# Ends of the modulation rounds at normal priority, and the recurrence's added products head beside head

## The chip, the cores and the metric

One core of a Trainium2 chip runs the whole program: two network blocks of two layers each, over 256 latent tokens (and 256 context tokens) of width 1024, all in f32. The metric is the device time of one execution in microseconds (us). Engines: PE (TensorE, matrix products; PEld is its weight load), DVE (VectorE), ACT (ScalarE), POOL (GpSimd), SP (SyncE, which issues most of the loads). The 16 DMA engines move data between memory and the core.

## The reference, cut to what matters

Every layer `i` of both blocks is steered by modulations: six rows of 1024 numbers, worked out from a conditioning vector with a weight of 1024 x 6144. The first layer's mixer holds a recurrence (RWKV-7) over the tokens, once forward and once backward, for eight heads of 64 x 64 state.

```
m_lat = jnp.split((c_lat_act @ w_ada[i] + b_ada[i])[:, None, :], 6, axis=-1)
m_ctx = jnp.split(c_ctx_act @ w_ada[i] + b_ada[i], 6, axis=-1)
...
def step(S, inp):
    r_t, w_t, k_t, v_t, a_t, b_t = inp
    sa = jnp.einsum('bhvk,bhk->bhv', S, a_t)
    S = S * w_t[:, :, None, :] + sa[..., None] * b_t[:, :, None, :] + v_t[..., None] * k_t[:, :, None, :]
    return S, jnp.einsum('bhvk,bhk->bhv', S, r_t)
```

The second block's layers use `ada_w` and `ada_b` in the same way. The four layers need 4 x 6 rows; a round makes two of them.

## The kernel before

**Modulations.** `ADA` lists 12 rounds, three for each of four layers: a round is `ada_round(i, r)`, and makes 2048 columns. It loads the weight in 8 steps of two buffers of 128 x 1024 (512 KB each, `raw`, five buffers in this part of the program), from SP's queue (`ada_load`, line 353). In each step four products of 128 x 512, side by side in four column strips of the array, add into one PSUM bank `ps` (line 377). Then comes the end of the round: the bank is added to a row tile `rows` that already holds the bias (line 380, DVE; the tile was cleared by POOL in line 364 and filled by line 373, SP); the sums go to memory as `mrows` for the later gates (line 383, ScalarE's queue; not for the rounds with r = 0); four transposes bring them into columns (line 386, PE) and four small copies into `mcol` (line 391, DVE). The banks of tag "A" hold both the sums and the transposes, and there is one of them; the row tile "adar" has one buffer too. So a round's products can't start before the end of the round ahead of it.

**Where the rounds run.** The first round runs at the start. The other eleven are written ahead of the recurrence (`in_proj`, lines 708 to 711): `filler(999)` issues them all, under `high_priority(offset=APRI)` with APRI = -100000, and then `rwkv()` is issued.

```
        s.fill = ADA[1:NADA]
        with s.tc.high_priority(offset=APRI):
            s.filler(999)
        s.run(s.rwkv())
```

The framework orders the instructions of each engine before the program runs: it follows a planned timeline, and of the instructions of an engine that are ready by it, it picks the one with the earliest place. `high_priority` moves that place forward by its offset; a negative offset moves it back. So the rounds' instructions stand behind all of the recurrence that is ready, and fill in where it is not. On the chip each engine then works through its fixed order, and waits where an operand is late. That goes for SP's queue of loads too, which also has the recurrence's own moves (lines 765, 768, 1018, 1022).

**The recurrence.** `rwkv` works on eight items: two halves of the tokens (th), two halves of those (sh), and two groups of four heads (u). `ORDER` gives their phases: P prepares (decays, keys, scores), I and Q invert small triangular blocks on DVE, C runs the chain `rw_chain`, F finishes. A chain has two steps, `rw_step` (line 1048), 16 in all; the two groups u don't depend on each other. `M` is the state, of the step before; it is absent in the first step of each group. A step has three stretches of products on PE, with copies on ACT and DVE between them:

- `zA`, first half (lines 1065 to 1071): for each direction d and half j, the products of M for both heads, then those of EA for both heads. They are 64 x 64, and stand at the rows of the array of one head and the columns of the other.
- `zA`, second half (lines 1077 to 1079).
- `z` (lines 1084 to 1090): for each d and j, and each of two heads h, a product with the full array from S and, where M is there, a 64 x 64 product from M that is added to half of the partitions of the same result.

All of a stretch lies in one PSUM bank. The step ends with `new = z + new` on DVE (line 1095). All `mm` calls are recorded under line 274; in the trace every f32 product of this kind shows as two instructions.

**Behind it.** `rw_end` and `mixer_out` (line 1369) split the results and project them; their loads stand behind the modulations' in SP's queue, and the gates that `mixer_out` needs are read back from `mrows` (line 414).

Of the kernel before, what the change touches and what calls it, by code (L numbers as in the profile page):

```python
# [12 lines left out]
ALU = mybir.AluOpType  # L13
# [41 lines left out]
APRI = -100000  # L55
# [10 lines left out]
class Builder:  # L66
# [205 lines left out]
    def mm(s, out, **kw):  # L272
        s.work += kw["rhs"].free_size() / (600 if kw["lhsT"].free_size() > 64 else 1200)
        s.nc.tensor.matmul(out, **kw)
# [85 lines left out]
    def ada_round(s, i, r):  # L360
        nc = s.nc
        act = s.act[i // 2]
        rows = s.row(nm="adar")
        nc.gpsimd.memset(rows, 0.0)
        while len(s.fraw) < 2:
            s.ada_load()
        ps = s.ps("ada")
        for k in range(8):
            s.ada_load()
            if k == 2:  # L370
                bsrc = s.I["b_ada" if i < 2 else "ada_b_2"][i % 2:i % 2 + 1, r * 2048:(r + 1) * 2048].rearrange("o (j f) -> (o j) f", j=4)
                for v in range(2):
                    nc.sync.dma_start(rows[v::32, :], bsrc)
            yield
            x = s.fraw.pop(0)
            for j in range(4):
                nc.tensor.matmul(ps[32 * j:32 * j + 32, :], lhsT=act[:, k, :], rhs=x[j // 2][:, j % 2 * 512:j % 2 * 512 + 512],  # L377
                                 start=(k == 0), stop=(k == 7), tile_position=(0, 32 * j))
            x = None
        nc.vector.tensor_tensor(rows, ps, rows, op=ALU.add)  # L380
        yield
        for v in range(0 if r == 0 else 2 if i == 0 else 1):
            nc.scalar.dma_start(s.mrows[i][r, :, v], rows[v::32, :])
        pt = s.ps("adat")
        for b in range(4):
            nc.tensor.transpose(pt[:, b * 128:(b + 1) * 128], rows[:, b * 128:(b + 1) * 128], s.ident)

        src = pt.rearrange("p (b j q) -> p b j q", b=4, j=4)[:, :, :, 0:2]
        dst = s.mcol[i][:, r * 16:(r + 1) * 16, :].rearrange("p (j b) i -> p b j i", j=4)
        for b in range(4):  # L390
            nc.vector.tensor_copy(dst[:, b], src[:, b])
        yield

    now = None

    def filler(s, n):

        while n or s.now:
            if s.now is None:
                if not s.fill and not s.rounds:  # L400
                    return
                s.now = s.ada_round(*(s.rounds or s.fill)[0])
            if next(s.now, s_end) is s_end:
                s.now = None
                s.rounds.pop(0)
            elif n:
                n -= 1
                if not n:
                    return
# [241 lines left out]
    def in_proj(s, xH, xL):  # L651
        nc, I = s.nc, s.I
        W = I["mix_w_in"]
        z13, t0, t1 = s.misc
        s.tl = [t0, t1]

        def ev(j, p):
            if j == 0:
                z12 = s.row(nm="z12")
                s.shift_mix(12, p, z12)  # L660
                for d in range(2):
                    for o in (32, 96):
                        nc.gpsimd.memset(s.tl[d][o:o + 1, :], 1.0)
                    nc.scalar.activation(s.tl[d][0:32, :], z12[32 * d:32 * d + 32, :], AF.Tanh)
                    nc.vector.tensor_copy(s.tl[d][64:96, :], z12[64 + 32 * d:96 + 32 * d, :])
            else:
                s.shift_mix(13, p, z13)

                nc.scalar.activation(z13[0:96, :], z13[0:96, :], AF.Tanh, scale=0.5)
                nc.gpsimd.tensor_scalar(z13[0:96, :], z13[0:96, :], 0.5, 0.5, op0=ALU.mult, op1=ALU.add)  # L670
        s.run(s.wstat2(I["wi_misc"], xH, xL, ev))
        s.z13 = z13
        s.rkv = {}
        s.rw_init()

        def krv_proj(half):
            for nm, o in (("k", 512), ("r", 0), ("v", 1024)):
                if nm == "k":
                    for th in range(2):
                        s.KR[th, half] = s.unit(nm="KR").rearrange("p (x j t) -> p x j t", x=2, j=2)  # L680
                if nm == "v":
                    t = s.rkv["v", half] = s.mx.tile([128, 2, 512], F32, name=s.n("rkv"))
                    z = lambda j: t[:, j]
                else:
                    z = lambda j: [s.KR[th, half][:, int(nm == "r"), j] for th in range(2)]
                yield from s.wstat2(W[:, o + half * 256:o + half * 256 + 256], xH, xL,
                                    lambda j, p: s.shift_mix(o // 128 + half * 2 + j, p, z(j)))
                if nm == "k":
                    s.rw_kk(half)

        s.xbc = [s.unit(nm="xbc").rearrange("p (a t) -> p a t", a=2) for _ in range(4)]
        s.xbc = [x[:, a] for x in s.xbc for a in range(2)]
        s.dump("@xbc")
        for c in range(4):
            s.run(s.wstat2(W[:, 2272 + c * 256:2272 + c * 256 + 256], xH, xL,
                           lambda j, p: s.conv5(c * 2 + j, p, s.xbc[c * 2 + j])))

        s.zg = [s.unit(nm="zg").rearrange("p (a t) -> p a t", a=2) for _ in range(2)]
        s.zg = [x[:, a] for x in s.zg for a in range(2)]

        def z_proj():
            yield from s.xstat(W, slice(1760, 2272), xH, xL, range(4), lambda t, p: nc.scalar.activation(s.zg[t], p, AF.Silu))
        s.dump("@weave")
        s.weave((s.hot(s.mamba(), HOTM), WB[0]), (s.chain(krv_proj(0), z_proj(), krv_proj(1)), WB[1]))
        xH = xL = None
        s.wstop()
        s.dump("@ada")
        s.fill = ADA[1:NADA]
        with s.tc.high_priority(offset=APRI):
            s.filler(999)  # L710
        s.run(s.rwkv())
        s.dump("@s7")
        s.rw_end()
# [334 lines left out]
    def rw_step(s, th, sh, u, i, new):  # L1048

        nc = s.nc  # L1050
        v, a, g = nc.vector, nc.scalar, nc.gpsimd
        mm = s.mm
        Y, M = s.YS[th, u], s.M[u]
        lc = (i, 1 - i)
        ch = (2 * sh + i, 3 - 2 * sh - i)
# [8 lines left out]
        AR, S, EA, UV = s.AR[th, sh, u], s.S[th, sh, u], s.EA[th, sh, u], s.UV[u]  # L1064
# [8 lines left out]
        if M is not None:  # L1073
            q = lambda x: x.rearrange("p h j d t -> p (h j d) t")
# [9 lines left out]
        z = s.ps("Z2").rearrange("p (h j d t) -> p h j d t", h=2, j=2, d=2)  # L1084
        for d, j in dj:
            for h in range(2):
                mm(z[:, h, j, d], lhsT=S[d][:, 2 * j + lc[d], 2 * h:2 * h + 2].rearrange("p e t -> p (e t)"), rhs=UV[:, j, ch[d], h], start=True, stop=True)
                if M is not None:
                    mm(z[BS[h], h, j, d], lhsT=AR[HS[h], d, j, lc[d], 1], rhs=M[HS[h], h, j, d], start=False, stop=True,
                       tile_position=(64 * h, 64 - 64 * h), skip_group_check=True)  # L1090
        f = lambda x: x.rearrange("p h j d t -> p (h j d t)")
# [1268 lines left out]
```

## Time and profile before

| | |
|---|---|
| timed runs (3) | 2815.34, 2804.44, 2808.48 us; median 2808.48 |
| profiled execution | 2815.26 us, span 2813.5 us |
| mean granted TensorE clock | 0.945 |
| instructions | 40633 |
| busy: PE, DVE, ACT, POOL | 93%, 67%, 46%, 6% of the span |

A busy share is a mean over stages that differ. The recurrence's stage lies between 250 and 690 us. A row of the trace has the start and the busy time in us, engine, line, operation and tiles (written <- read); "Z" is the tile of `zA` and `z`, "YM" that of M, "UV" and "S" are the operands of the full products, "EA" that of the other half-size ones.

### The profile page before, as it was taken

What the parts mean: (1) busy time and instruction counts of PE and PEld (TensorE: products, weight loads), DVE (VectorE), ACT (ScalarE), POOL (GpSimd) and SP (SyncE); (2) the same over time, 40 slices, a digit from 0 to 9 for tenths busy, and PEclk for the clock granted to TensorE, in tenths of its full rate; (3) what the DMA queues carried; (4) which work ended last, traced back from release to release, by engine and by line L of the source; (5) the groups of instructions that cost most, each with busy time, mean ns of one, the idle gap of its engine ahead of it and who ended that gap; (6) DMA issues with size and microseconds to landing.
All of it is one profiled execution on the core that took longest, in us unless ns stands there. A gap on an engine that the chain in (4) does not pass through costs nothing. (4 is left out here: it accounts for less than half of the span.)

```text
span 2813.5 us, 40633 instructions
## 1 busy us (share of the span) xinstructions
PE 2623.4 (93%) x15434; PEld 2094.0 (74%) x15434; DVE 1885.7 (67%) x3039; ACT 1287.7 (46%) x1760; POOL 171.5 (6%) x276
## 2 busy tenths in 40 slices
PE   6999899997999998999999999999998987997798
PEld 3776456553888887887788888888876866996797
DVE  4657877833634448456798988898896566555655
ACT  3532122111432223444688777777775443443343
POOL 0112222210000000000000000000000000000000
PEclk8999887887999999999899999999999998998899
DMA  6224776667433333333599999999996324653552
GB/s 238 87 75 161 271 242 195 205 212 276 136 97 98 98 91 105 85 111 112 207 369 349 343 346 344 364 362 340 359 343 238 122 92 148 189 186 99 162 183 75
DMA packets 324444, 570.83 MB, mean 203 GB/s; under 512 B 61752, under 2 KB 167608, under 8 KB 324240
## 3 DMA queue, kind: packets, MB, share of 16 engines
q1 hardware_dynamic: 304064, 544.61, 56.4%
q10 hardware_dynamic: 16784, 11.74, 1.4%
q0 software_dynamic: 3392, 11.80, 1.2%
q8 instruction: 123, 2.02, 0.3%
q14 instruction: 81, 0.66, 0.1%
HBM read 563.79 MB, written 4.28 MB: 202 GB/s over the span
## 5 line engine op out<-in xcount | busy, mean ns | idle before, releaser
L204 DVE TENSOR_TENSOR wl<-raw,wh 128x1024 fp32r<-128x1024 f32 x828 | 984.7, 1222 | 421.7 <-ACT wh L203 401.9
L203 ACT CAST wh<-raw 128x1024 fp32r<-128x1024 f32 x828 | 838.7, 1050 | 506.6 <-issue 191.7
L249 PE MATMUL ws<-xL,wh 128*128 128x256 f32 (+1 forms) x1392 | 456.3, 328 | 3.7 <-DVE xL L204 3.7
L248 PE MATMUL ws<-xH,wh 128*128 128x256 f32 (+1 forms) x1392 | 458.1, 331 | 0.8 <-DVE xTf L482 0.5
L250 PE MATMUL ws<-xH,wl 128*128 128x256 f32 (+1 forms) x1392 | 457.3, 329 | 0.9 <-DVE wl L204 0.9
L249 PE MATMUL mw<-wl,eH 128*128 128x512 f32 (+1 forms) x768 | 289.7, 377 | 1.4 <-DVE wl L204 1.2
L248 PEld LDWEIGHTS ws<-xH,wh 128*128 128x128 f32 x1392 | 265.3, 191 | 33.3 <-issue 7.8
L249 PEld LDWEIGHTS ws<-xL,wh 128*128 128x128 f32 x1392 | 265.1, 190 | 30.7 <-DVE xL L204 4.8
L248 PE MATMUL mw<-wh,eH 128*128 128x512 f32 (+1 forms) x768 | 286.1, 375 | 1.8 <-ACT wh L203 1.8
L250 PEld LDWEIGHTS ws<-xH,wl 128*128 128x128 f32 x1392 | 265.1, 190 | 29.7 <-issue 5.3
L250 PE MATMUL mw<-wh,eL 128*128 128x512 f32 (+1 forms) x768 | 286.2, 373 | 0.0
L377 PE MATMUL ada<-raw,act 128*32 128x512 f32 x768 | 175.0, 731 | 35.2 <-DMA raw<-in_w_ada 14.3
L249 PEld LDWEIGHTS mw<-wl,eH 128*128 128x128 f32 x768 | 145.0, 189 | 33.2 <-DVE wl L204 8.9
L248 PEld LDWEIGHTS mw<-wh,eH 128*128 128x128 f32 x768 | 144.9, 189 | 28.2 <-ACT wh L203 3.1
L250 PEld LDWEIGHTS mw<-wh,eL 128*128 128x128 f32 x768 | 145.0, 189 | 24.0
L249 PE MATMUL y<-wl,uH 128*128 128x512 f32 x352 | 139.6, 397 | 2.0 <-DVE wl L204 2.0
L250 PE MATMUL y<-wh,uL 128*128 128x512 f32 x352 | 135.7, 391 | 0.0
L248 PE MATMUL y<-wh,uH 128*128 128x512 f32 x352 | 115.0, 390 | 0.0
L471 PE MATMUL xT<-ident,xn 128*128 128x128 f32 x160 | 36.0, 403 | 82.8 <-DVE xn L449 51.5
L377 PEld LDWEIGHTS ada<-raw,act 128*32 128x32 f32 x768 | 28.2, 122 | 108.1 <-issue 37.7
L248 PE MATMUL o<-wh,mH 128*128 128x512 f32 x256 | 100.0, 390 | 0.0
L249 PE MATMUL o<-wl,mH 128*128 128x512 f32 x256 | 99.9, 390 | 0.0
(483 smaller groups left out, 4066.4 us busy)
## 6 DMA issues: line engine op xcount, KB each, us to landing
raw<-in_moe_w SPq DMA_DIRECT2D x528, 512.0 KB
raw<-in_mlp_w SPq DMA_DIRECT2D x128, 512.0 KB
raw<-in_w_ada SPq DMA_DIRECT2D x96, 512.0 KB
raw<-in_ada_w SPq DMA_DIRECT2D x96, 512.0 KB
raw<-in_ffn_w SPq DMA_DIRECT2D x66, 512.0 KB
raw<-in_mix_w_in SPq DMA_DIRECT2D x24, 512.0 KB
raw<-in_na_w_qkv SPq DMA_DIRECT2D x24, 512.0 KB
raw<-in_w_in SPq DMA_DIRECT2D x24, 512.0 KB
```

The costliest lines, as they stand in the source:

```text
L203: s.nc.scalar.copy(H, raw)
L204: s.nc.vector.tensor_tensor(L, raw, H, op=ALU.subtract)
L248: mm(out, lhsT=lH, rhs=rH, start=start, stop=False)
L249: mm(out, lhsT=lH, rhs=rL, start=False, stop=False)
L250: mm(out, lhsT=lL, rhs=rH, start=False, stop=stop)
L377: nc.tensor.matmul(ps[32 * j:32 * j + 32, :], lhsT=act[:, k, :], rhs=x[j // 2][:, j % 2 * 512:j % 2 * 512 + 512], start=(k == 0), stop=(k ...
L471: nc.tensor.transpose(p[:, j, t * 128:t * 128 + 128], xn[t][:, k * 128:k * 128 + 128], s.ident)
```

## The change

In `z` the two heads' products from S are issued first, and then the two from M; only the first product of the bank carries the flag that starts it. In `ada_round` the addition, the row DMAs, the transposes and the copies stand under `high_priority` with an offset of `roundpri`, which is -APRI while the eleven rounds are issued (so that the two offsets cancel) and 0 otherwise.

```diff
+        with s.tc.high_priority(offset=s.roundpri):
+            nc.vector.tensor_tensor(rows, ps, rows, op=ALU.add)
         yield
+        with s.tc.high_priority(offset=s.roundpri):
+            for v in range(0 if r == 0 else 2 if i == 0 else 1):
+                nc.scalar.dma_start(s.mrows[i][r, :, v], rows[v::32, :])
+            pt = s.ps("adat")
+            for b in range(4):
+                nc.tensor.transpose(pt[:, b * 128:(b + 1) * 128], rows[:, b * 128:(b + 1) * 128], s.ident)
...
+            for b in range(4):
+                nc.vector.tensor_copy(dst[:, b], src[:, b])
         yield
...
+    roundpri = 0
...
+        s.roundpri = -APRI
         with s.tc.high_priority(offset=APRI):
             s.filler(999)
+        s.roundpri = 0
...
             for h in range(2):
-                mm(z[:, h, j, d], lhsT=S[d][:, 2 * j + lc[d], 2 * h:2 * h + 2].rearrange("p e t -> p (e t)"), rhs=UV[:, j, ch[d], h], start=True, stop=True)
-                if M is not None:
+
+                mm(z[:, h, j, d], lhsT=S[d][:, 2 * j + lc[d], 2 * h:2 * h + 2].rearrange("p e t -> p (e t)"), rhs=UV[:, j, ch[d], h],
+                   start=(d, j, h) == (0, 0, 0), stop=True, skip_group_check=True)
+
+            if M is not None:
+                for h in range(2):
                     mm(z[BS[h], h, j, d], lhsT=AR[HS[h], d, j, lc[d], 1], rhs=M[HS[h], h, j, d], start=False, stop=True,
                        tile_position=(64 * h, 64 - 64 * h), skip_group_check=True)
```

## Rows read from the trace of the kernel before

**Rows 1.** The page: busy time of PE; GB/s in 40 equal slices of the span.

```profile
PE 2623.4 (93%) x15434; PEld 2094.0 (74%) x15434; DVE 1885.7 (67%) x3039; ACT 1287.7 (46%) x1760; POOL 171.5 (6%) x276
...
GB/s 238 87 75 161 271 242 195 205 212 276 136 97 98 98 91 105 85 111 112 207 369 349 343 346 344 364 362 340 359 343 238 122 92 148 189 186 99 162 183 75
```

**Rows 2.** Stretches: length, busy PE, PEld, DVE, ACT, POOL; clock, DMA share, GB/s.

```profile
600.00:645.00 45.00, 44.69 (x432) 26.72 (x432) 13.79 (x37) 4.12 (x10) 7.82 (x10) 0.81 0.67 228
645.00:688.00 43.00, 27.46 (x127) 7.86 (x127) 13.10 (x35) 6.00 (x8) 4.19 (x6) 0.74 0.73 246
268.00:688.00 420.00, 380.01 (x3589) 218.80 (x3587) 272.29 (x898) 77.99 (x161) 93.70 (x162) 0.83 0.68 226
...
516.00:518.00 2.00, 2.00 (x9) 1.59 (x9) 0.41 (x1) 0.00 (x0) 0.00 (x0) 0.50 0.00 0
```

**Rows 3.** Groups by line, 268 to 688: busy, mean ns | idle before, releaser.

```profile
L377 PE MATMUL ada<-raw,act 128*32 128x512 f32 x642 | 145.9, 744 | 23.8 <-DMA raw<-in_ada_w 12.5 <-DMA raw<-in_w_ada 9.5 <-issue 1.5
...
L274 PE MATMUL Z<-UV,S 128*128 128x64 f32 x256 | 58.9, 325 | 0.4 <-DVE UV L1081 0.4
L274 PE MATMUL Z<-YM,AR 64*64 64x64 f32 x448 | 57.9, 258 | 0.0
```

**Rows 4.** Waits of SP's queue, 268 to 688: us in total, times, longest.

```profile
SPq L353 <- PE ada L377: 193.7, 86, 10.0
...
SPq L373 <- DMA mrows<-adar: 8.8, 2, 4.5
```

**Rows 5.** Timeline of PE, 508 to 525: a step's products, a round's end.

```profile
511.73 0.43 PE L274 MATMUL Z<-UV,S 128*128 128x64 f32 x2
512.09 0.33 PE L274 MATMUL Z<-YM,AR 64*64 64x64 f32 x2
512.35 0.43 PE L274 MATMUL Z<-UV,S 128*128 128x64 f32 x2
...
516.47 0.69 PE L274 MATMUL Z<-UV,S 128*128 128x64 f32 x2
...
517.49 2.07 PE L274 MATMUL sc<-AR,bk 64*128 64x128 f32 x8
519.49 0.90 PE L386 MATMUL adat<-ident,adar 128*128 128x128 f32 x3
...
523.85 1.94 PE L377 MATMUL ada<-raw,act 128*32 128x512 f32 x8
```

**Rows 6.** Timeline of DVE, 508 to 523: the same round's addition and copies.

```profile
510.76 0.69 DVE L380 TENSOR_TENSOR adar<-ada,adar 128x512 f32<-128x512 f32 x1 [0.16 <-PE ada L377]
...
522.42 0.30 DVE L391 COPY mcol<-adat 128x8 f32<-128x8 f32 x3
```

**Rows 7.** Timeline of PE, 345 to 351: products from S alone; products of zA.

```profile
345.49 1.90 PE L274 MATMUL Z<-UV,S 128*128 128x64 f32 x16
347.22 0.61 PE L278 MATMUL bt<-ident,bk 128*128 128x128 f32 x4
...
349.03 0.28 PE L274 MATMUL Z<-YM,AR 64*64 64x64 f32 x4
349.15 0.28 PE L274 MATMUL Z<-UV,EA 64*64 64x64 f32 x4
```

**Rows 8.** Timeline of all engines, 645 to 715: the end of the stage.

```profile
671.07 1.22 DVE L204 TENSOR_TENSOR oL<-rkv,oH 128x1024 fp32r<-128x1024 f32 x1 [1.11 <-ACT oH L203]
...
679.09 0.69 DVE L380 TENSOR_TENSOR adar<-ada,adar 128x512 f32<-128x512 f32 x1 [6.80 <-DMA raw<-in_mix_w_out]
...
679.84 0.66 PE L386 MATMUL adat<-ident,adar 128*128 128x128 f32 x4 [0.85 <-DVE adar L380]
...
685.03 2.23 POOL L414 DMA_DIRECT2D gate<-mrows  x3 [28.96 <-DMA mrows<-adar]
...
687.93 2.04 PE L248 MATMUL xs<-wh,oH 128*128 128x512 f32 x4 [7.44 <-ACT wh L203]
```

**Rows 9.** Waits of all engines, 250 to 685: us in total, times, longest.

```profile
DVE iv L1012 <- DMA E<-dsc: 11.0, 6, 3.9
```

More of the change, by code (lines that the diff above doesn't have):

```diff
@@ L379, in ada_round @@
             x = None
-        nc.vector.tensor_tensor(rows, ps, rows, op=ALU.add)
+        with s.tc.high_priority(offset=s.roundpri):
+            nc.vector.tensor_tensor(rows, ps, rows, op=ALU.add)
         yield
[L382 to L391, printed above, removed]
+        with s.tc.high_priority(offset=s.roundpri):
[4 more added lines that the diff above has]
+                nc.tensor.transpose(pt[:, b * 128:(b + 1) * 128], rows[:, b * 128:(b + 1) * 128], s.ident)
+            src = pt.rearrange("p (b j q) -> p b j q", b=4, j=4)[:, :, :, 0:2]
+            dst = s.mcol[i][:, r * 16:(r + 1) * 16, :].rearrange("p (j b) i -> p b j i", j=4)
+            for b in range(4):
+                nc.vector.tensor_copy(dst[:, b], src[:, b])
         yield
     now = None
+    roundpri = 0
     def filler(s, n):
```

## The prediction

> **What bounds the kernel now.** I began with the page: TensorE is busy for 93% of the span [rows 1], so anything that shortens another engine alone is worth little, and the question is what PE does where the change lies. Both edits act in one stretch, the recurrence (`rwkv`) with the modulations' rounds filling in between. The stretches' view bounds it: from 268 us (end of the first of the eleven rounds that `filler(999)` issues) to 688 us (the first product of the stage behind) it lasts 420 us, 15% of the span. PE is busy for 380.0 of them, DVE for 272.3, and the DMA engines for 0.68 of the time [rows 2]. PE is the fullest, and more so late: 44.69 of 45 us between 600 and 645. The 40 us in which it is idle fall into 24.5 before 645 and 15.5 after (43.0 less 27.46).
>
> The groups by line say what PE does there: 145.9 us of modulation products (`ada`), and about 59 and 58 us in products of the recurrence that write `Z` from `S` and from `M` (their tile is named YM) [rows 3]; the latter hold also those of `zA`, which are not touched. The waits say that the loads of the modulations stand 193.7 us for PE to free a buffer [rows 4], far more than PE's own wait for them (12.5 and 9.5 us, in [rows 3]). So in this stretch PE's queue, in its written order, sets the pace, and the loads follow. Only from 645 on is it the other way round: the recurrence's last value is split at 671.07, while the last round is added at 679.09, its rows come back from memory for the gates at 685.03, and PE starts the next stage at 687.93 [rows 8].
>
> **Part by part: the recurrence's products.** `rw_step` runs 16 times, 14 of them with a state `M` (one addition of line 1095 each). Such a step issues, for each of four pairs (direction, half), S of head 0, M of head 0, S of head 1, M of head 1; every f32 product stands in the trace as two instructions. That is the alternation S x2, M x2 of [rows 5]: eight per step, 112 in all. One takes 0.62 us from start to start (511.73 to 512.35): 0.36 until M starts, 0.26 until the next S. 27 of the 112 run at 1.02 us (516.47 to 517.49 is one), where the granted clock is 0.50, the lower level of 1.2 GHz [rows 2]; 85 run at 0.62.
>
> The edit makes it S x4, M x4 per pair. Two prices are shown elsewhere in the same stage. Sixteen S without an M between take 345.49 to 347.22, 0.11 us each [rows 7]; so the second head's two S add 0.22 to the 0.36, 0.58 in all. Of the M: in `zA` the products of both heads already stand side by side, at the same positions in the array (rows of one head, columns of the other); four of them pass in 0.12 us (349.03 to 349.15). The second head's pair there starts with the first's, so four M cost what two cost now, 0.26. A pair of heads then takes 0.84 in place of 1.24, 0.40 less; I take 0.39 for the offset between the two starts. Other end: if the two heads' M ran one behind the other they would cost at most twice 0.26, the pair 1.10, and the saving would be 0.14, all of it from S no longer changing places with M. A loss on PE itself is excluded: same instructions, fewer changes of shape, no wait for another engine added. I take the upper value, because its row has the same shape, the same two positions and one bank.
>
> The Trainium skill (TensorEngine Tiling, Gotcha 1: PSUM Pressure) states that different row tiles can't access one PSUM bank at the same time; both heads' M read different rows of the array and write one bank, so by it the saving would be the 0.14. The trace does not bear that out where it can be seen: the four of `zA` lie in one bank too, and pass in 0.12.
>
> Sum: 112 alternations are 56 pairs, 42.5 at full and 13.5 at half clock. 42.5 x 0.39 = 16.6 us; at half clock the saving grows as the alternation does (1.02/0.62), 13.5 x 0.64 = 8.7 us; together 25.3 us, other end 0.14/0.39 of it, 9 us. On the path: before 645 PE is idle for 24.5 of 377 us, so what PE is spared nearly all moves the stretch. I take 20 of the 25, the rest being lost where the freed time meets products whose weights have not landed.
>
> **The rounds' ends.** Eleven rounds run under `high_priority(offset=APRI)`, behind all other work that is ready. The edit brings the end of each to the place that it has in the program, ahead of the recurrence: one DVE addition (0.69), one or two row DMAs on ScalarE's queue, four transposes, four small copies (0.30 for three of them). Nothing is added. What it moves is seen in the worst of the rounds: added at 510.76, its transposes are issued at 519.49, behind a whole step of the recurrence and eight score products, its copies end at 522.72, and the next round starts at 523.85 [rows 5, 6]. Over the eleven, transposes start 30 us behind the start of their additions in sum, from 8.7 here to 0.75 in the last round (679.09 to 679.84, [rows 8]); at 0.75 each it would be 8, so 22 us of lateness can go. The bank that holds a round is one, and so is the row tile, which the next round's bias load needs back: SP stood 8.8 us for that row's DMAs [rows 4], with weight loads queued behind it. So the rounds, and their loads, can come up to 22 us earlier against the recurrence.
>
> That is not 22 us of time. While PE is full, a round that comes earlier pushes the recurrence back by as much. It pays only where PE is idle: after 645, where it waits for the last round's loads. Of the 15.5 idle us there, 7.4 lie between the last round's transposes and 687.93, and some such tail stays in any order; 8 can go, and perhaps a few of the 24.5 before. I take 5. On the other side, the moved work takes DVE 11 x 1.1 = 12 us ahead of other work; DVE is idle for a third of the stretch, which hides it, and 12 us is the price without that. ScalarE's queue gets its row DMA earlier, and waits there for the addition; it is busy for 78 of 420 us. SP's loads move up with the rounds: this is the rival below. What is late next when the rounds no longer are: the last values of the recurrence, at 671 less the 20.
>
> Sum: 20 + 5 = 25 us. The profiled execution took 2815.26 us (span 2813.5), the upper end of the three timed runs; against it that gives 2790, and against their median of 2808.48, which is what a timing should show, 2783.5.
>
> **Rivals.** (A) The heads' M pass one after the other: 9 us instead of 25, at 0.8 on the path 7, with 5 for the rounds: 2796. For it: in `zA` all products are of one shape, while here S fills the whole array before. Against it: the four M follow each other all the same.
>
> (B) The loads bound the stage once PE is spared. For it: PE's idle time is nearly all before `ada` products, 22 us of it on DMA [rows 3], and DMA is at 0.68, 0.73 at the end [rows 2]. If every second microsecond saved becomes a wait there, 20 turn to 10 and the rounds bring nothing: 2798. Against it: 226 GB/s over the stretch, while the page shows 340 and more in others [rows 1].
>
> (C) Slower: SP's queue. It is one row of loads in written order, and the recurrence's own moves (the blocks' E, the inverse's X, 16 places) stand in it between weight loads that wait for PE, up to 10.0 us at a time [rows 4]. With the rounds moved up, weight loads are written ahead of those moves; if PE is later than was planned, each move waits, DVE's inverse waits for it (11.0 us in six waits today, longest 3.9 [rows 9]), and the chain of steps with it. At 1.6 us per place, 25 us, the gain is gone; at the 3.9 of today's longest it is 62, less 25: 37 slower, 2846; half way, 2822 to 2826. Against it: PE is full, so a late chain is first filled by modulation work.
>
> (D) The order does not come out as written, because the instructions of an engine are picked by readiness in a planned timeline: M of head 0 first waits for its S. Today's order is exactly the program's in spite of the same dependence [rows 5], so I give it little; it would leave 5 us, 2803.
>
> **Chances.** Forecast (2768 to 2794) 0.57; A 0.10; B 0.15; C 0.12; D 0.06. A change within 0.5%, 14 us, can't be told from none. Of the forecast's share all but 0.02 lies below 2794.4; A gives 0.04 there, B 0.04: faster 0.63. Slower takes the larger part of C and nothing else, 0.09; the same 0.28. The range runs from 2768 (all 25.3 on the path, and 15 from the rounds) to 2810 (D, and C where it just balances).
>
> **What would show it.** In the timeline of a step, S x4 and M x4 with about 0.84 us from S to S; S x2, M x2 would refute the order, 1.10 the overlap. Transposes within 2 us of each round's last product; the last round's addition before, not 8 us behind, the last split of the recurrence; the first product of the next stage near 663 in place of 688. SP's wait before the E and X moves must not grow, nor DVE's on E: that would be C. PE's idle time ahead of `ada` growing by 10 us or more would be B. The prediction fails if the stretch from 268 to 688 shortens by less than 14 us, or if time moves in the stages behind it, which the edits don't touch.

## The result, and the profile after

The changed kernel takes 2772.98 us (median of 4 runs, 2770.54 to 2774.14) against 2806.46 for the kernel before beside it (2802.32 to 2815.34): a ratio of 0.9871, interval 0.9849 to 0.9894, so 33.5 us less where 25 were forecast, and inside the forecast of 2768 to 2794. The profiled execution took 2774.14 us, the one of before 2815.26, the upper end of its runs; the two profiles therefore differ by more (41 us) than the medians.

First the page, then the stretch that the forecast was about, from the end of the first round to the first product of the stage behind (columns as in [rows 2]):

```profile
PE 2575.4 (93%) x15434; PEld 2066.5 (75%) x15434; DVE 1885.3 (68%) x3039; ACT 1286.5 (46%) x1760; POOL 172.4 (6%) x276
```

```profile
270.40:647.00 376.60, 331.00 (x3587) 191.07 (x3587) 271.65 (x898) 77.44 (x161) 95.09 (x162) 0.91 0.75 253
```

The stretch has shrunk from 420.0 us [rows 2] to 376.6 with the same number of instructions to within two; from its end to the end of the program it is 2125.3 us now and was 2125.6. So all of the change lies here. PE is busy for 49 us less (380.0 to 331.0), idle for 45.6 in place of 40.0. And one number stands beside the busy times that the forecast left alone: the granted clock, 0.83 before and 0.91 now. With two levels, 1.2 and 2.4 GHz, a mean of 0.83 over 420 us is 142 us at the lower one, and 0.91 over 376.6 is 66 (both from the clock unrounded).

The groups of the same stretch say whose time went (busy, mean ns of one, idle before and its releasers):

```profile
L377 PE MATMUL ada<-raw,act 128*32 128x512 f32 x642 | 132.4, 650 | 19.9 <-DMA raw<-in_ada_w 10.2 <-DMA raw<-in_w_ada 8.9 <-PE et L274 0.4
L274 PE MATMUL Z<-UV,S 128*128 128x64 f32 x256 | 42.2, 288 | 1.4 <-DVE UV L1086 1.0 <-ACT UV L1086 0.5
L274 PE MATMUL Z<-YM,AR 64*64 64x64 f32 x448 | 35.7, 244 | 0.9 <-DVE YM L1104 0.9
```

The products from S and M, which the change reorders, lost 16.7 and 22.2 us against [rows 3]. But `ada`, of which the change alters neither instructions nor shapes, lost 13.5 as well: each of its products is 94 ns shorter. The records overlap, so these sums aren't to be added to the microsecond.

In the timeline of PE, a step with a state now reads:

```profile
356.77 0.66 PE L274 MATMUL Z<-UV,S 128*128 128x64 f32 x4 [0.16 <-DVE UV L1086]
357.36 0.33 PE L274 MATMUL Z<-YM,AR 64*64 64x64 f32 x4
357.62 0.66 PE L274 MATMUL Z<-UV,S 128*128 128x64 f32 x4
358.21 0.33 PE L274 MATMUL Z<-YM,AR 64*64 64x64 f32 x4
```

S x4 and M x4, 0.85 us from S to S (356.77 to 357.62). 49 of the 56 pairs stand like that, the others with other products in between; only one of the 49 runs at the lower clock.

A round's end is still not always prompt. The one of the greatest delay, in the timeline of PE:

```profile
483.32 1.05 PE L377 MATMUL ada<-raw,act 128*32 128x512 f32 x4 [1.46 <-DMA raw<-in_ada_w]
485.75 1.29 PE L274 MATMUL m<-EA,X 32*32 32x32 f32 x32 [1.38 <-DVE X L1041]
486.98 2.08 PE L274 MATMUL bo<-bon,cmix 128*128 128x512 f32 x2
488.98 2.07 PE L274 MATMUL sc<-AR,bk 64*128 64x128 f32 x8
490.99 1.11 PE L388 MATMUL adat<-ident,adar 128*128 128x128 f32 x4
```

The round's last product ends at 484.37, and its transposes start 6.6 us later, behind three other groups. Over the eleven rounds the delay from addition to transposes adds up to some 18 us, where it was 30.

The end of the stage, in the timeline of all engines:

```profile
633.46 0.68 DVE L381 TENSOR_TENSOR adar<-ada,adar 128x512 f32<-128x512 f32 x1
634.20 0.66 PE L388 MATMUL adat<-ident,adar 128*128 128x128 f32 x4 [1.86 <-DVE adar L381]
...
643.78 2.23 POOL L417 DMA_DIRECT2D gate<-mrows  x3 [11.90 <-DVE rkv L1153]
...
644.31 1.23 DVE L204 TENSOR_TENSOR oL<-rkv,oH 128x1024 fp32r<-128x1024 f32 x1 [1.17 <-ACT oH L203]
...
646.99 1.22 PE L248 MATMUL xs<-wh,oH 128*128 128x512 f32 x2 [4.57 <-ACT wh L203]
```

The last round is added at 633.46, 10.8 us ahead of the recurrence's last split; before it came 8.0 us behind [rows 8]. The recurrence ends last now, and the next stage starts 2.7 us behind its split, no longer 16.9. The waits of SP's queue, and of DVE for E, show no jam:

```profile
SPq L353 <- PE ada L377: 149.9, 81, 13.3
...
SPq L373 <- DMA mrows<-adar: 5.0, 1, 5.0
```

```profile
DVE iv L1017 <- DMA E<-dsc: 12.1, 6, 5.0
```

The weight loads still stand mostly for PE (193.7 before [rows 4]), the rounds' row holds SP for 5.0 us in place of 8.8, and DVE's wait has gone from 11.0 [rows 9] to 12.1.

### The profile page after: what moved, and what is told of

The parts are those of the page before. It is cut to its first block, busy times and chain, and to the rows that moved or that the text cites. A ratio compares the mean times of both kernels' runs of the same rounds, so it can differ in the third digit from the quotient of the medians.

```text
span 2772.3 us, 40625 instructions
## 1 busy us (share of the span) xinstructions
PE 2575.4 (93%) x15434; PEld 2066.5 (75%) x15434; DVE 1885.3 (68%) x3039; ACT 1286.5 (46%) x1760; POOL 172.4 (6%) x276
## 5 line engine op out<-in xcount | busy, mean ns | idle before, releaser
L248 PEld LDWEIGHTS ws<-xH,wh 128*128 128x128 f32 x1392 | 265.9, 192 | 33.5 <-issue 7.8
L377 PE MATMUL ada<-raw,act 128*32 128x512 f32 x768 | 162.6, 658 | 32.3 <-DMA raw<-in_w_ada 14.4
L250 PE MATMUL o<-wh,mL 128*128 128x512 f32 x256 | 98.6, 389 | 0.0
```

Source lines behind the costliest of these rows:

```text
L248: mm(out, lhsT=lH, rhs=rH, start=start, stop=False)
L250: mm(out, lhsT=lL, rhs=rH, start=False, stop=stop)
```

## The experiments

Two theories were open after this. By the first, PE is spared work by the order of the products, and nothing else counts. By the second the clock has a part of its own: the alternation of shapes also brings it down, for what stands behind it too. The rounds' ends were the third candidate. The runs stand here by what they answer; e1 to e4 came first, then b2, a2, e5 and e6, then e7 to e9.

**One part of the change at a time.** The kernel before with the products' part of the diff alone, and the changed kernel with the old products, so the rounds' ends alone:

```
e1_products: before.py +   for d, j in dj:
                               for h in range(2): mm(S)
                               if M is not None:
                                   for h in range(2): mm(M)
e2_ends:     before.py +   with s.tc.high_priority(offset=s.roundpri): ...   (both blocks)
```

> The products' order alone; the ends of the rounds stay at low priority. Theory 1, PE's own time: 56 pairs at 0.39 us less, 20 us faster than before (about 2786), the mean granted clock between the first round's end and the next stage stays near 0.83. Theory 2, the clock: what the alternation of full and half-size products cost beyond its own time was the granted clock; the stretch's clock rises to about 0.91 as in the changed kernel, and 28 to 33 us go (about 2775 to 2779). Theory 3, the ends: at most 10 us (2796 or more), since the rounds still end late.

> The ends of the rounds at normal priority alone; the products alternate as before. Theory 1: 5 us faster (about 2801). Theory 2: 0 to 5 us, with 10 or more of the 14 steps followed by a fall of the clock as before, and a mean clock near 0.83. Theory 3: 15 us or more (2791 or less), with the weight loads waiting less.

Products alone: 2776.21 us against 2809.4, ratio 0.9885 [0.9861, 0.9909]. That is where the second theory put it. Ends alone: 2807.98, ratio 0.9996 [0.9977, 1.0015], which is between 6.5 us less and 4.2 more. The stretches of the two:

```profile
272.80:647.20 374.40, 330.37 (x3587) 193.37 (x3586) 271.52 (x898) 77.52 (x161) 95.83 (x162) 0.90 0.75 253
```

```profile
268.90:685.70 416.80, 382.34 (x3587) 222.29 (x3587) 270.14 (x898) 77.53 (x161) 95.05 (x162) 0.82 0.69 228
```

With the ends alone PE's idle time falls from 40.0 to 34.5 us, and the last round is added at 672.06, 10.8 us ahead of the recurrence's split at 682.91: the tail that the forecast wanted gone is gone. Still the next stage starts at 685.67, in an execution as long as the profiled one of before (2815.01 and 2815.26 us): the recurrence's split has moved from 671.07 to 682.91, and PE's busy time has risen from 380.0 to 382.3 at a clock of 0.82. The priority has traded the rounds' lateness for the recurrence's. With the products alone, in the timeline of DVE, the last round's addition and the last split:

```profile
633.54 0.68 DVE L380 TENSOR_TENSOR adar<-ada,adar 128x512 f32<-128x512 f32 x1
...
644.33 1.23 DVE L204 TENSOR_TENSOR oL<-rkv,oH 128x1024 fp32r<-128x1024 f32 x1 [1.17 <-ACT oH L203]
```

They stand 10.8 us apart, as in the changed kernel, and over the eleven rounds the delay from addition to transposes is 17.8 us, where the changed kernel has 17.9. So the late last round went with the products, and the ends' priority, put on top of them, hardly moved a round. The whole change has 0.9871, and 0.9858 in a second measurement (a2_after, below), 4 and 8 us less than 0.9885; the intervals overlap, the traces show nothing that such a gain could come from, and whether there is one stays open.

**What the order costs on PE, and what side by side adds.** All eight S first, then all eight M, the heads alternating, or head by head:

```
e3_all_s_first: for d, j in dj:  for h in range(2): mm(S)
                for d, j in dj:  for h in range(2): mm(M)
e4_m_by_head:   as e3, but    for h in range(2): for d, j in dj: mm(M)
```

> The changed kernel with all eight S products of a step first and then all eight from M: one change of shape per step each way in place of four. Theory 1: a step takes about 2.5 us on PE (16 x 0.11, a change of 0.2, 16 at 0.03) in place of 3.4, so 14 x 0.9 = 12 us less, about 2761. Theory 2: the clock has little left to give in these steps (3 of 14 still end in a fall), so also 8 to 15 us less. Rival: the M products now all wait for the last S, and the next step's sum comes no earlier; within 3 us of the changed kernel.

> As the kernel with all S first, but the M products in order of head: all eight records of head 0, then all eight of head 1, so that the two heads' are not beside each other. Overlap theory: head by head they pass at 0.1 us each, 16 x 0.1 = 1.6 us where they passed in 0.5 side by side, a step is 1.1 us longer, 14 steps 15 us: no faster than the changed kernel. If only the changes of shape mattered: the same as the kernel with all S first, within 2 us.

A step in the timeline of PE, of e3 and then of e4:

```profile
504.64 2.00 PE L274 MATMUL Z<-UV,S 128*128 128x64 f32 x16
506.57 0.68 PE L274 MATMUL Z<-YM,AR 64*64 64x64 f32 x16
507.18 1.04 PE L274 MATMUL sc<-AR,bk 64*128 64x128 f32 x7
```

```profile
508.11 2.00 PE L274 MATMUL Z<-UV,S 128*128 128x64 f32 x16
510.04 0.96 PE L274 MATMUL Z<-YM,AR 64*64 64x64 f32 x16
510.93 1.16 PE L274 MATMUL sc<-AR,bk 64*128 64x128 f32 x8
```

From the first S to the next group it is 2.54 us in e3 and 2.82 in e4, where the changed kernel needs 3.40 (four times 0.85) and the kernel before 4.96 (eight times 0.62). So side by side is worth 0.28 us a step, 0.07 a pair, where 1.1 a step was expected; the rest of what is spared is that PE changes shape less often. Yet both are slower than the changed kernel, against what was expected of e3 by either theory: 2796.06 us (0.9962 [0.9943, 0.9982]) and 2802.05 (0.9970 [0.9953, 0.9986]). PE's gain doesn't arrive. Where it stays, e3 shows, first in the products of `ada` on PE, then in SP's queue:

```profile
448.10 1.05 PE L377 MATMUL ada<-raw,act 128*32 128x512 f32 x4 [0.70 <-DMA raw<-in_ada_w]
...
474.46 1.05 PE L377 MATMUL ada<-raw,act 128*32 128x512 f32 x4
```

```profile
444.08 5.44 SPq L353 DMA_DIRECT2D raw<-in_ada_w  x5
459.75 0.82 SPq L770 DMA_DIRECT2D dsc<-EA  x2
461.83 1.13 SPq L773 DMA_DIRECT2D E<-dsc  x2
475.55 0.36 SPq L353 DMA_DIRECT2D raw<-in_ada_w  x1
```

In the order that was written out for PE, no modulation product stands between 448 and 474 us, though the five buffers are full; so none comes free, and SP issues no weight load for 26 us. The rounds fall behind, and at the stage's end, in the timeline of all engines, PE has to wait for them again:

```profile
640.13 1.23 DVE L204 TENSOR_TENSOR oL<-rkv,oH 128x1024 fp32r<-128x1024 f32 x1 [1.11 <-ACT oH L203]
...
651.42 0.69 DVE L381 TENSOR_TENSOR adar<-ada,adar 128x512 f32<-128x512 f32 x1 [10.06 <-DMA raw<-in_mix_w_out]
...
660.38 1.19 PE L248 MATMUL xs<-wh,oH 128*128 128x512 f32 x2 [7.56 <-ACT wh L203]
```

The recurrence is done 4 us sooner than in the changed kernel (640.13 against 644.31), the last round 18 us later, and PE is idle for 66.2 us of the stretch.

**The order of the kernel before without the change of shape.** S, M, S, M as before, with each M product read over the whole array:

```
e7_full_m: before.py, with
    mm(z[:, h, j, d], lhsT=AR[:, d, j, lc[d]].rearrange("p e t -> p (e t)"),
       rhs=M[:, h, j, d], start=False, stop=True, skip_group_check=True)
```

> The kernel before, in its own alternating order S, M, S, M, but with each M product of a step made over the whole array (128 rows and 128 columns, both heads' rows and both e at once; the sum is then not the reference's). Nothing changes shape any more, the products and their order stay. If it is the change of shape that costs the time and lets the clock fall: 32 records at 0.11 us, 3.6 us a step, at most 4 of 14 steps with a fall of the clock, and about the time of the changed kernel (2770 to 2785). If it is the order (a product added right behind the one it adds to): 5 us a step, 9 or more falls, 2800 to 2815.

In the timeline of PE:

```profile
502.12 0.39 PE L274 MATMUL Z<-YM,AR 128*128 128x64 f32 x2
502.34 0.39 PE L274 MATMUL Z<-UV,S 128*128 128x64 f32 x2
502.57 0.39 PE L274 MATMUL Z<-YM,AR 128*128 128x64 f32 x2
```

S and M take 0.22 us each now, 0.45 for what took 0.62, in the same order and with products that use more of the array. On PE the price was the change of shape: 3.6 us a step, as expected. The whole kernel takes 2790.46 us, ratio 0.9946 [0.9924, 0.9969], between the two times that were expected, since as in e3 the rounds end late (the last added at 652.14) and PE is idle for 56.3 us. Its stretch:

```profile
270.90:661.30 390.40, 334.05 (x3586) 200.78 (x3586) 275.82 (x898) 77.30 (x161) 95.13 (x162) 0.92 0.72 243
```

The clock is 0.92, though every S still has its M behind it.

The order of PE's queue is planned anew for each kernel, so the times of whole kernels also hold what their orders cost; the time of a step on PE and the clock are read apart from that.

**The clock.** The kernel before was profiled a second time (b2_before, 2801.12 us), and the changed one too (a2_after).

> The kernel before once more, for a second profile of it: the first was taken in an execution 7 us above its median. The stretch from the first of the eleven rounds to the next stage should be 410 to 417 us in place of 419.5, with 7 or more of the 14 steps ending at the lower clock, if the clock's fall belongs to the kernel and not to that execution.

> The changed kernel again, beside the two below. 0.986 to 0.989 of the kernel before. Beside the products' order alone (0.9885 of before) it tells what the ends are worth on top of it: theory 1, 5 us, 0.9867; theory 2, under 3 us, 0.9875 or more.

a2_after has a median of 2774.32 us, ratio 0.9858 [0.9832, 0.9884]. The stretch of before in its two profiles, then of the second profile of after (an execution of 2786.7 us):

```profile
268.40:687.90 419.50, 379.54 (x3586) 218.59 (x3586) 272.19 (x898) 77.89 (x161) 93.70 (x162) 0.83 0.68 226
269.30:672.70 403.40, 366.64 (x3586) 208.55 (x3587) 272.38 (x898) 78.02 (x161) 93.30 (x162) 0.87 0.70 235
```

```profile
271.60:656.40 384.80, 338.14 (x3587) 195.75 (x3586) 271.31 (x898) 77.28 (x161) 94.45 (x162) 0.89 0.73 247
```

The same kernel in the same order differs by 16 us in this stretch from one execution to the next (419.5 and 403.4, less than the 410 that were expected at least), and with it the time at 1.2 GHz, 142 and 107 us: 0.46 us for each. For the changed kernel it is 8.2 us for 22, 0.37. Where the clock falls, steps of before show, in its second profile; the stretches are one step and what stands right behind it:

```profile
422.60:430.00 7.40, 7.40 (x41) 6.07 (x40) 4.29 (x19) 0.30 (x1) 0.51 (x1) 0.73 0.86 259
441.40:449.00 7.60, 7.60 (x77) 5.14 (x80) 7.41 (x21) 0.71 (x2) 1.98 (x11) 0.84 0.39 140
457.90:465.00 7.10, 7.10 (x73) 5.65 (x72) 5.83 (x17) 0.99 (x2) 3.09 (x4) 0.91 0.58 199
```

By its records PE isn't idle for a moment in them, and the clock falls in each (the column ahead of the DMA share). In the changed kernel, in its first profile:

```profile
422.20:427.00 4.80, 4.80 (x41) 3.95 (x40) 2.86 (x12) 0.59 (x1) 0.41 (x1) 1.00 0.97 282
437.80:444.00 6.20, 6.20 (x68) 3.96 (x68) 5.30 (x14) 0.00 (x0) 0.00 (x0) 0.79 0.99 389
451.60:458.00 6.40, 6.40 (x85) 5.42 (x88) 4.74 (x17) 1.09 (x3) 2.82 (x3) 1.00 0.40 104
```

One of three. Counted over the 14 steps, with a fall of the clock between a step's start and 2 us behind its end: 12 and 13 in the two profiles of before and 11 with the ends alone, which all alternate; 3, 2 and 3 in the changed kernel's two and the products alone; 1 each in e3 and e4; none in e7. The first theory leaves this out; the second says it.

Steps are not the only place where it falls. In the whole stretch it does so 22 and 21 times in before and 17 with the ends alone; 9 and 10 times in the two profiles of after and 10 with the products alone. Of these, 9, 10 and 6 have no idle time of PE in the 7 us before them (under 0.05 us), all at alternating steps, against 1, 0 and 2; in e3, e4 and e7 every fall has some idle time ahead of it. So nearly all of the falls at a busy PE belong to the alternation; the others come behind idle time, in every kernel.

**Is it the length of a step, not the shapes?** The changed kernel with every S product issued twice in these steps:

```
e5_s_twice: for again in range(1 if M is None else 2):
                mm(S, start=(d, j, h, again) == (0, 0, 0, 0))
```

> The changed kernel, but in the 14 steps with a state each S product is issued twice, so that its part of the sum is doubled. That makes a step some 5.2 us on PE at full clock (8 more products of two records at 0.11 us, 1.8 us), as long as the alternation of the kernel before at full clock (4.96), but without its changes of shape. If the length of the step in itself lets the clock fall: 8 or more of 14 steps end at the lower clock, and the time goes back to that of the kernel before, 2805 or more. If it is the alternation, with the engine standing between shapes: 0 to 3 falls, a stretch clock near 0.9, and no more than the added products' own time, 14 x 1.8 = 25 us, 2798 or less.

In the timeline of PE:

```profile
431.91 1.10 PE L274 MATMUL Z<-UV,S 128*128 128x64 f32 x8
432.95 0.33 PE L274 MATMUL Z<-YM,AR 64*64 64x64 f32 x4
```

A step takes 5.2 us, a little longer than the 4.96 of before, and the clock falls at 1 of 14. So it isn't the length. All in all this kernel takes 2811.33 us (1.0010 [0.9986, 1.0034]), 37 us above the changed one, for 24.6 us of products (14 x 16 x 0.11). That misses the 2798 expected if the alternation is the cause, and is the time that was expected of the other case. Its stretch shows why the time doesn't settle it:

```profile
269.10:692.60 423.50, 371.11 (x3811) 232.09 (x3810) 274.42 (x898) 78.29 (x161) 95.00 (x162) 0.87 0.66 224
```

As in e3, its written order leaves a hole, of 44.7 us without a modulation product ahead of the eighth round, the last round is added at 683.53, and PE is idle for 52.4 us. The clock is 0.87, no better than in the second profile of before: 113 us at 1.2 GHz. But all of its 10 falls come behind idle time of PE, and none at a busy PE as in before.

**Better orders?** Per direction, four S and then four M; and the changed kernel and e3 with the rounds planned earlier:

```
e6_by_direction:  for d: (for j, h: mm(S));  (for j, h: mm(M))
e8_rounds_sooner: after.py with APRI = -2000
e9_all_s_sooner:  e3 with APRI = -2000
```

> Between the changed kernel and the one with all S first: for each direction four S products, then its four M products; two changes to M per step in place of four or one. On PE about 2.8 us per step in place of 3.4. If PE's time alone counts: 14 x 0.6 = 8 us faster than the changed kernel, 2765. If what made the kernel with all S first slower, in spite of its shorter steps, is that the modulations' rounds fall behind in the written order (its round 7 took 66 us) and the next stage waits for the last of them: the rounds end later than 640 us, and it lands between the two, 2775 to 2796.

> The changed kernel with the rounds set back by 2000 places and not by 100000, so that in the second half of the recurrence they go ahead of work that is ready. The changed kernel's last round is added 13 us ahead of the recurrence's last split, so the recurrence sets the end: if PE's total work decides, no gain, 2768 to 2780; if the recurrence is pushed back by what the rounds take, 5 to 15 us slower.

> The kernel with all S first, with the rounds set back by 2000 places. There the last round was added 10 us behind the recurrence's last split and PE was idle for 66 us of the stretch. If the late rounds are what made it slower than the changed kernel: 15 to 30 us faster than it was (2796), 2766 to 2781. If its slower time lies in the order of the recurrence itself: 2790 to 2800.

2795.78 us (0.9939 [0.9917, 0.9962]), 2783.07 (0.9923 [0.9901, 0.9946]) and 2797.55 (0.9966 [0.9945, 0.9987]). e6 has no fall of the clock at its steps at all, and PE is idle for 72.1 us of its stretch, the most of all; its rounds end late, and its time is the one expected of that. In e8 PE is idle about as long as in the changed kernel; its recurrence ends 6.6 us later (split at 650.94), the case in which 5 to 15 us of loss were expected. In e9 the rounds still end last (659.11, split 649.88), so it doesn't tell late rounds from the recurrence's own order. None beats the changed kernel. Why the planner writes a hole in e3, e5 and e6 wasn't found out.

## Why the prediction was right, and where its sizes were off

**The bound.** PE's queue in its written order set the pace: with the products alone PE's busy time falls by about 50 us and the stretch by 45. That held.

**The pair.** 0.84 us was forecast, 0.85 measured, and the order came out as written, which refutes rival D. The reason given for the bounds was wrong, though. The lower end, a saving of 0.14, took a second head's M to cost another 0.26 us. In e4 the M of one head, with no S between, start 0.058 us apart, and head by head costs 0.07 a pair more than side by side: so the second head's M behind the first's would still have saved some 0.32 (an estimate from these rows). Of the 0.26, two M at that spacing are 0.12; the rest goes with the change of shape. Rival A is refuted by the 0.85 us; its price, 0.26 a pair, was too high by e3 against e4. The Trainium skill (TensorEngine Tiling (Array Packing), Gotcha 1: PSUM Pressure), weighed in the forecast, isn't borne out: the M of two heads, different row tiles writing different partitions of one bank, start 7 ns apart in the changed kernel. The same page (Key Properties) says "Mode switching requires drain", without a price; the traces agree that a change of shape costs time, with 205 ns from S to M and 148 back, where two S stand 112 apart.

**The term that was mis-sized: the clock.** The forecast took 13.5 of the 56 pairs to stay at 1.2 GHz, and gave the rest of PE's work its old speed. In fact the time at 1.2 GHz fell with the alternation, from 142 and 107 us in the two profiles of before to 66 and 88 in the two of after. By the means of the two (124 to 77 us) and the 0.37 to 0.46 us that each cost between executions of one kernel, 18 to 22 us of the some 31 by which the stretch shortened (411.5 to 380.7) are the clock's, 9 to 13 PE's own time: an estimate from two profiles of each. By PE's busy time it looks alike: that fell by 38.5 us on the mean, of which the forecast's 21.8 us for the pairs leave some 17 to the clock, and PE's idle time grew by 8. The forecast had 21.8 us of PE's own time (56 x 0.39) and 3.5 more for the pairs at the lower clock, and put 20 of the 25 on the path. So its total for the products, against the 33 that e1 measured (25.6 to 39.1 by its interval), came out too small by a term that it didn't have. Its own term was too large on the path: if all of the added idle time is put down to it, about half of what PE is spared reaches the end of the stage. That the time came out inside the forecast is in part luck: PE's own 9 to 13 us alone would have given some 2793 to 2797, at the forecast's upper edge and where rival A stood. What the runs show is that the falls of the clock at a busy PE come with the alternation of shapes (e1, e2, e7) and aren't tied to the length of the step (e5). By what the chip decides on it they don't show.

**The rounds.** 5 us were forecast, and no run shows them. By itself (e2) the edit brought the last round 10.8 us ahead of the last split, as forecast, and gave nothing: PE being full, a round that comes earlier pushes the recurrence back, as the forecast said of the stretch before 645 and then left out of its tail. In the changed kernel the same 10.8 us aren't the edit's work, for the products alone have them too (e1). "Transposes within 2 us of each round's last product" was wrong for several rounds (6.6 at most): in PE's written order other groups still stood ahead of them.

**Rivals B and C.** PE's idle time ahead of `ada`, B's sign, fell from 23.8 to 19.9 us; in all its idle time grew by 5.6, and the DMA share rose to 0.75. (The 23.8 were also not "nearly all" of the idle time before, which was 40.0.) C's signs are all but absent in the changed kernel (SP's wait before the E and X moves is 50 us where it was 51, its wait for PE fell to 149.9, DVE's for E rose by 1.1), but something of its kind held e3, e5 and e6 back: rounds and loads that come late because of where they were written, DVE waiting 16.4 us for E in e3. The forecast tied it to rounds that are moved up. What sets it off isn't shown: e3 and e6 have shorter steps than the changed kernel, e5 longer ones.

**The end.** The next stage was forecast near 663, and starts at 647, in the second profile at 656.4; by the estimate above the clock's part is what the forecast lacked. Behind it nothing moved (2125.6 and 2125.3), as named.

## What to carry to other kernels

Where small TensorE products of two shapes alternate, read the time from start to start at each change of shape and group the products by shape: here an alternation took 0.62 us, of which its four products at the spacing that they have among their own kind (0.11 and 0.058 us) are some 0.34, and parallel positions in the array hardly counted (0.07 us of 0.85 a pair). Read the granted clock of the stretch before and after any such edit, and of two profiles of the same kernel: here 0.91 against 0.83 was, by estimate, worth about as much as the time that the products themselves were spared. And where the order of the queues is planned ahead, the shortest sequence on the bounding engine needn't be the fastest (e3): look for holes in what feeds the loads.

## What the runs showed of the hardware that was not expected

- Where full-array and 64x64 products alternate, the granted clock falls in or right behind 11 to 13 of 14 steps, at 6 to 10 of them with no gap of PE in the records of the 7 us before; with the same number of products grouped by shape, or all of the full shape in the same order, it does so at 0 to 3 (at 1 in e5, with steps as long as those of before).
- Products of 64x64, 64 columns wide, that follow each other start 0.058 us apart in the records (e4, but for the first two), and two of them every 0.058 where they alternate between two positions (e3); full-array ones stand 0.11 apart.
- Single runs of the kernel before spread by over 20 us on one chip (2799.68 to 2821.06), and the two profiles put 16 us of such a difference into this stretch, with the clock.
